# A hybrid encoder: q and k prepared for two token tiles at once, and GpSimd's large products given to VectorE

## The chip, the cores and the metric

The kernel runs on one core of a Trainium2 chip. The metric is the device time of the whole program in microseconds (us). A core has five engines that matter here, each with its own queue that it works through in order: TensorE (PE in the profile: matrix products and transposes; PEld is its loading of weights), VectorE (DVE), ScalarE (ACT), GpSimd (POOL) and SyncE (SP), which issues all of this kernel's transfers between HBM and the on-chip memory SBUF. TensorE writes its results into PSUM, from where VectorE and ScalarE read them.

## The reference, cut to what matters

Two layers act on a residual stream x of 512 tokens by 1024 columns, all in float32. A layer normalizes x, scales and shifts it by vectors made from the conditioning c, and multiplies it by w_in (1024 x 3712). The columns of that product feed three branches:

- A, differential attention: 4 heads with two softmax maps each over 32 columns of q and k, 64 columns of values;
- B, dilated window attention: 6 heads of 64 columns, with the three windows folded into one mask over 512 keys;
- C, retention: 4 heads, 48 columns of q and k, 96 of values, in chunks of 128 tokens, in both directions.

Each branch is multiplied by a SiLU gate, the three are joined and multiplied by w_out, and the result, times a gate made from c, is added to x. What the change touches is above all the preparation of q and k in A and B:

```
qa = rope(rms_norm(qa.reshape(B, S, H_A, 2, DK_A), qn_a[l]), ROT_THETA, ROT_A)
qb = rope(rms_norm(qb.reshape(B, S, H_B, DH_B), qn_b[l]), ROT_THETA, ROT_B)
```

That is: a root mean square over each head's 32 or 64 columns, a division by it, and a rotation of the first quarter of the columns. k goes the same way.

## The kernel before, in words

**Tiling.** The tokens lie in 4 tiles of 128 (`NT`), one token to a partition. Weights come in pieces of two blocks of 128 rows (`Piece`). Each is split into two parts whose sum is the float32 number: ScalarE writes the first part (`whi`), VectorE subtracts to get the second (`wlo`, L307), and three products replace one (`products`, L329). Products of one chunk of columns go group by group: one group is one weight piece with one token tile, six products; 16 groups make a chunk (`in_chunk`, L419) with four accumulating PSUM buffers, one for each token tile.

**The units.** A and B are worked through in units of two or four heads with 128 columns of q, of k and of values (`Unit`, L573): A0, B0, A1, B1, B2 in each layer, so 10 units in all, 4 of A (32 columns, 8 heads of q and k in a tile) and 6 of B (64 columns, 4 in a tile). When the 16 groups of a unit's chunk end, `done` (L580) copies q and k of a token tile into a buffer `qkraw` of 256 columns. Then three steps follow for each token tile:

- `norm` (L601): ScalarE squares the tile into `qkn`; VectorE sums each head (L608) and brings in 1/n and the epsilon (L570); GpSimd raises to the power -1/2 (L198, reached through `rms_end` and `pow_half`). VectorE forms two rotary products (L616, L617) and their sum (L618), in place in `qkraw`.
- `scale` (L620): GpSimd multiplies the 256 columns by the powers, broadcast over the head, into `qkn` (L622).
- `turn` (L625), for two tiles at once: TensorE transposes four blocks of 128x128 into the one PSUM buffer for turns (`tr4`, L552), ScalarE and VectorE empty it into `nat`.

When all four tiles are done, `stack` (L638) moves `nat` by transfers into the layout in which the scores read q and k. `Attention` (L665) and its two kinds, `Diff` (L704) and `Dilated` (L771), then make scores, Exp, softmax weights, turns of these and the products with the values; `finish2` to `finish4` (L743 to L769) end a unit of A: turn back, square (L748, GpSimd), sum, power, scaling (L762), gating (L764, GpSimd), turn again.

**Retention.** `rope` (L891) forms one rotary product on GpSimd (L896), one on VectorE (L898), and the sum on GpSimd (L899); `sums` and `norm` (L960, L965) take sums, power and scaling.

**The end of a layer.** `out_done` (L1110) multiplies a tile of the output product by the gate and adds x: in layer 0 on GpSimd for the first half of the columns and on VectorE for the second (L1117). `h_all` (L1087) makes the next layer's input, two pieces of 256 columns at a time.

**What sets the order.** The author's plan is a list of groups (`groups`), each of which may have steps bound to it (`at`, L163): a step named at group g is written behind group g's products. The constants in L33 to L51 are distances in groups: `NORM` 1, `SCALE` 5, `TURN` 6 after the last group of a token tile. This gives the order in which the program is written. The framework then makes each engine's queue: the order written is its priority, but an instruction that it takes to be ready may be put ahead of an earlier one. Two places are held: `high_priority` around the products with the values, and `tc.keep_in_program_order` in `sums` and `norm` of retention, which ties an instruction behind the one written before it on its engine. Once made, a queue is fixed, and an instruction that waits holds up everything behind it on its engine.

**Buffers.** A pool gives each tag a number of buffers. `qkraw` has 4 of 256 columns; the norm gains of the next layer (`mod_gain`, L477) share them. `qkn` has two tags with 2 each, which `h_tile` (L562) shares.

Of the kernel before, what the change touches and what calls it, by code (L numbers as in the profile page):

```python
# [48 lines left out]
E_T1, E_T2, E_X, E_QF, E_SCALE_A, E_SCALE_B = 1, 1, 1, 0, 0, 0  # L49
# [84 lines left out]
def encoder(ctx, tc, x, c, norm_g, w_ada, b_ada, w_in, w_out, params, consts, out):  # L134
# [5 lines left out]
    four = pool("four", 4)  # L140
# [421 lines left out]
    def h_tile(t, q, rstd):  # L562
        f = slice(q * 256, q * 256 + 256)
        hn = two.tile([P, 256], F32, name="hn", tag=f"qkn{q % 2}")
        stt(hn, x_sb[t][:, f], rstd[t], mods[q][:, 256:], OP.mult, OP.mult)
        V.tensor_tensor(hn, hn, mods[q][:, :256], OP.add)
        return hn
# [5 lines left out]
    class Unit:  # L573
# [6 lines left out]
        def done(self, t, ps, g0):  # L580
            if t == 0:
                self.v = three.tile([P, NT, P], F32, name="v")
                if self.gated:
                    self.ga = two.tile([P, NT, P], F32, name="ga")
            n, ng_ = self.n, 256 // self.n
            raw = self.raw[t] = four.tile([P, 256], F32, name="qkraw")
            act(raw, ps[:, 0:256])
            act(self.v[:, t], ps[:, 256:384])
            if self.gated:
                th = one.tile([P, P], F32, name="th")  # L590
                act(th, ps[:, 384:512], AF.Tanh, scale=0.5)
                stt(self.ga[:, t], th, 1.0, ps[:, 384:512], OP.add, OP.mult)
            g = g0 + 12 + t
            at(g + NORM, self.norm, t)
            at(g + SCALE, self.scale, t)
            if t % 2:
                at(g + TURN, self.turn, t // 2)
            if t == NT - 1:
                at(g + STACK, self.stack)

        def norm(self, t):  # L601
            n, ng_ = self.n, 256 // self.n
# [8 lines left out]
            ct_, st_ = tabs[n]  # L611
            r3 = raw.rearrange("p (g n) -> p g n", n=n)
# [7 lines left out]
        def scale(self, t):  # L620
            n, ng_ = self.n, 256 // self.n
            (V if (E_SCALE_A if n == DK_A else E_SCALE_B) % 2 else G).tensor_tensor(self.qn[t], self.raw[t].rearrange("p (g n) -> p g n", n=n),  # L622
                            self.ss[t].unsqueeze(2).to_broadcast([P, ng_, n]), OP.mult)

        def turn(self, i):  # L625
            if i == 0:
                self.nat = [[one.tile([P, S], F32R, name=f"nat{w}{z}", tag=f"nat{2 * w + z}") for z in range(2)] for w in range(2)]
            q2 = [self.qn[2 * i + j].rearrange("p g n -> p (g n)") for j in range(2)]
            ps = tr4([q2[j][:, w * P:(w + 1) * P] for w in range(2) for j in range(2)])
# [74 lines left out]
    class Diff(Attention):  # L704
# [38 lines left out]
        def finish2(self, g):  # L743
# [4 lines left out]
            G.tensor_tensor(sq, o, o, OP.mult)  # L748
# [10 lines left out]
        def finish3(self):  # L759
# [4 lines left out]
            G.tensor_tensor(on, on, self.u.ga, OP.mult)  # L764
# [6 lines left out]
    class Dilated(Attention):  # L771
        def __init__(self, unit, g0, gap, ob, sg, out):
            self.ob, self.sg, self.out = ob, sg, out
            self.s = {}
            super().__init__(unit, g0, gap, sg is not None)
# [6 lines left out]
        def scores(self, qt):  # L782
            for h in range(2):
# [7 lines left out]
                s_ = self.s[h] = sm.tile([P, 1], F32, name="bs")  # L791
                act(sb, sb, AF.Exp, bias=mx, scale=-1.0, accum_out=s_)

        def soft(self, qt):
            for h in range(2):
                V.reciprocal(self.s[h], self.s[h])
                sb = self.e[qt, h]
                if h == 0 or qt >= N_SOFT:
                    act(sb, sb, AF.Copy, scale=self.s[h])
                else:  # L800
                    V.tensor_scalar(sb, sb, self.s[h], None, OP.mult)
# [28 lines left out]
    class Retention:  # L830
# [60 lines left out]
        def rope(self, t):  # L891
# [22 lines left out]
        def turn_f(self, t):  # L914
            (V.tensor_copy if E_QF % 2 else act)(self.qfT[:, :, tok_(t)], tr4([self.fq[:, h] for h in range(4)]))
# [69 lines left out]
    def layer(l):  # L985
# [101 lines left out]
        def h_all(t, q):  # L1087
            hn = [h_tile(t, q + j, rstd_next) for j in range(2)]
            ps = tr4([hn[j][:, k * P:(k + 1) * P] for j in range(2) for k in range(2)])
# [8 lines left out]
        for hf in range(2):  # L1098
# [11 lines left out]
            def out_done(t, ps, cols, hf):  # L1110
# [5 lines left out]
                else:  # L1116
                    (V if hf * E_X % 2 else G).tensor_tensor(x_sb[t][:, cols], y, x_sb[t][:, cols], OP.add)  # L1117
# [181 lines left out]
```

## Time and profile before

| What | us |
|---|---|
| median of 3 runs (lowest, highest) | 652.2 (651.58, 652.81) |
| the profiled execution's own time | 653.0 |
| its span, first to last instruction | 651.2 |
| busy: PE | 625.5 |
| busy: PEld | 514.2 |
| busy: DVE | 496.8 |
| busy: ACT | 340.2 |
| busy: POOL | 164.4 |

The mean granted clock of TensorE is 0.989 of full speed. How to read the profile: "busy" is the time in which an engine had an instruction under way; an engine that is not the last to finish loses nothing by its idle time. A row of instructions names the source line, the engine, the operation, what is written and read, the shape (partitions x columns), the count, the busy time and the mean duration, then the idle time of the engine in front and who ended it. L155 and L158 are helpers through which many calls go; there the names of the tiles tell them apart. The chain of waits is followed back from the last instruction, at each step to what released it.

### The profile page before, as it was taken

The page shows a single profiled execution, that of the slowest core. Times are in us where ns is not written, and L with a number is a line of the kernel's source. Part 1 is how long each engine was busy: PE and PEld are TensorE (multiplying, and loading weights), DVE is VectorE, ACT ScalarE, POOL GpSimd, SP SyncE. Part 2 cuts the span into 40 slices and gives each one's busy share as a digit, 9 for nine tenths or more (in the row PEclk, how much of TensorE's full clock was granted, in tenths as well). Part 3 has the DMA queues.
Part 4 walks back from the last instruction along what each step waited for, and adds up shares of the span by engine and source line. Part 5 has one row for each costly group of instructions (what it writes and reads, how often), then busy time and mean ns, then how long its engine had stood idle before and what let it go on. Part 6 is the DMA issues. An engine that isn't in the chain of part 4 may idle for free.

```text
span 651.2 us, 10473 instructions
## 1 busy us (share of the span) xinstructions
PE 625.5 (96%) x3487; PEld 514.2 (79%) x3487; DVE 496.8 (76%) x1212; ACT 340.2 (52%) x750; POOL 164.4 (25%) x183
## 2 busy tenths in 40 slices
PE   6999999999999996999999999999999999899997
PEld 1878888987888873677779998997788787677786
DVE  1889776789978986997869374778997996677543
ACT  4744362666746665564434244455756567656410
POOL 1105462514360510200411041632323340010000
PEclk9799999999999998999999999999999999999999
DMA  9987123426565557476643322235555453603211
GB/s 315 334 290 207 40 82 88 133 91 152 147 177 167 125 172 175 141 254 224 185 169 96 90 72 67 77 101 154 142 171 137 142 142 103 163 32 139 89 64 65
DMA packets 87133, 93.03 MB, mean 143 GB/s; under 512 B 7044, under 2 KB 68132, under 8 KB 87080
## 3 DMA queue, kind: packets, MB, share of 16 engines
q1 hardware_dynamic: 87080, 92.37, 47.8%
q8 instruction: 28, 0.46, 0.3%
q14 instruction: 25, 0.20, 0.1%
HBM read 72.42 MB, written 4.19 MB: 118 GB/s over the span
## 4 chain that ended last, share of the span: by engine, by line
PE 77%; DVE 11%; issue 5%; POOL 3%; DMA 2%; ACT 2%; SPq 0%; POOLq 0%; ACTq 0%; DVEq 0%
PE acc L338 15%; PE acc L340 15%; PE acc L339 15%; PE tr L555 8%; PE pv L701 5%; PE sc L724 2%; PE acc L334 2%; PE acc L335 1%; PE acc L336 1%; DVE ada_acc L158 1%; PE sc L785 1%; DVE wlo L307 1%; PE sc L786 1%; PE line L519 1%; PE co L954 1%
## 5 line engine op out<-in xcount | busy, mean ns | idle before, releaser
L338 PE MATMUL acc<-whi,hT 128*128 128x384 f32 (+1 forms) x424 | 155.1, 366 | 0.0
L339 PE MATMUL acc<-wlo,hT 128*128 128x384 f32 (+1 forms) x424 | 152.3, 359 | 0.0
L340 PE MATMUL acc<-whi,hL 128*128 128x384 f32 (+1 forms) x424 | 152.0, 358 | 0.0
L307 DVE TENSOR_TENSOR wlo<-raw,whi 128x384 fp32r<-128x384 f32 (+1 forms) x130 | 81.8, 658 | 27.0 <-ACT whi L155 26.7
L198 POOL TENSOR_TENSOR qkss<-qkss,nhalf 128x4 f32<-128x4 f32 (+1 forms) x40 | 52.6, 1316 | 128.3 <-DVE qkss L570 125.7
L338 PEld LDWEIGHTS acc<-whi,hT 128*128 128x128 f32 x424 | 79.9, 188 | 6.1
L340 PEld LDWEIGHTS acc<-whi,hL 128*128 128x128 f32 x424 | 79.8, 188 | 6.2
L339 PEld LDWEIGHTS acc<-wlo,hT 128*128 128x128 f32 x424 | 79.9, 188 | 5.5
L155 ACT ACTIVATE whi<-raw 128x768 fp32r<-128x768 f32 (+2 forms) x67 | 59.6, 890 | 36.8 <-PE acc L340 34.0
L158 DVE SCALAR_TENSOR_TENSOR ada_acc<-raw,cs,ada_acc 128x512 f32<-128x512 f32 x86 | 64.4, 750 | 7.1 <-DMA raw<-in_w_ada_dram 5.9
L155 ACT ACTIVATE e<-sc,mx 128x512 f32<-128x512 f32 x64 | 43.9, 688 | 35.8 <-DVE mx L726 17.2
L726 DVE TENSOR_REDUCE mx<-sc 128x1 f32<-128x512 f32 x64 | 43.5, 685 | 9.6 <-PE sc L724 9.1
L155 ACT ACTIVATE sb<-sb,mx 128x512 f32<-128x512 f32 x48 | 34.4, 717 | 20.5 <-DVE mx L790 20.2
L701 PE MATMUL pv<-pt,v 128*64 128x256 f32 x320 | 40.1, 394 | 0.6 <-DVE pt L691 0.5
L155 ACT ACTIVATE pt<-tr 128x512 f32<-128x512 f32 x40 | 23.8, 596 | 24.2 <-PE tr L555 24.1
L790 DVE CUSTOM_DVE_ANT_0 sb<-sc,cst 128x512 f32<-128x512 f32 x48 | 32.1, 684 | 5.4 <-PE sc L786 3.5
L555 PE MATMUL tr<-cst,sb 128*128 128x128 f32 x192 | 30.5, 282 | 5.3 <-DVE nat L158 2.2
L701 PEld LDWEIGHTS pv<-pt,v 128*64 128x64 f32 x320 | 21.7, 140 | 16.6 <-DVE pt L691 5.3
L555 PEld LDWEIGHTS tr<-cst,sb 128*128 128x128 f32 x192 | 22.1, 142 | 15.8 <-ACT pt L155 7.3
L691 DVE COPY pt<-tr 128x512 f32<-128x512 f32 x40 | 27.4, 684 | 8.4 <-PE tr L555 8.4
L622 POOL TENSOR_TENSOR qkn<-qkraw,qkss 128x256 f32<-128x256 f32 x40 | 30.4, 760 | 5.8 <-DVE qkraw L618 2.0
L724 PE MATMUL sc<-stk,stq 96*128 96x512 f32 x64 | 27.3, 434 | 0.9 <-ACT e L155 0.9
(293 smaller groups left out, 1368.9 us busy)
## 6 DMA issues: line engine op xcount, KB each, us to landing
raw<-in_w_ada_dram SPq DMA_DIRECT2D x64, 256.0 KB, 4.8
raw<-in_w_in_dram SPq DMA_DIRECT2D x48, 192.0 KB, 2.6
raw<-in_w_in_dram SPq DMA_DIRECT2D x24, 384.0 KB, 3.9
raw<-in_w_in_dram SPq DMA_DIRECT2D x32, 256.0 KB, 3.6
raw<-in_w_ada_dram SPq DMA_DIRECT2D x16, 512.0 KB, 5.4
raw<-in_w_out_dram SPq DMA_DIRECT2D x32, 256.0 KB, 2.8
x<-in_x_dram SPq DMA_DIRECT2D x8, 512.0 KB, 3.5
stB<-nat SPq DMA_DIRECT2D x32, 128.0 KB, 2.3
```

The source lines that it names most:

```text
L155: A.activation(o, i, f, **kw)
L158: V.scalar_tensor_tensor(o, a, s, b, op0, op1)
L198: G.tensor_tensor(o, i, nhalf[:, :n], OP.pow)
L307: V.tensor_tensor(l2[:, z], r2[:, z], h2[:, z].bitcast(F32), OP.subtract)
L338: T.matmul(ps, ah, hi[i], start=s_, stop=False)
L339: T.matmul(ps, ah, lo[i], start=False, stop=False)
L340: T.matmul(ps, al, hi[i], start=False, stop=e_)
L555: T.transpose(ps[:, i, :], b, ident)
L701: T.matmul(self.pv[h * 64:h * 64 + 64, i * 256:i * 256 + 256], self.u.v[:, k, h * 64:h * 64 + 64], self.pt[h][:, k], start=k == 0, stop=k ...
L724: T.matmul(ps, self.u.stq[0:96, m, tok_(qt)], self.u.stk[0:96, m], start=True, stop=True)
L726: V.tensor_reduce(mx, ps, AX.X, OP.max, negate=True)
L790: V.tensor_tensor_reduce(sb, ps, cst[:, m0:m0 + S], 1.0, 3e38, OP.add, OP.min, mx)
```

## The change

Three things are done. First, `norm` and `scale` of a unit take two token tiles at a time: `qkraw` and `qkn` are tiles of two times 256 columns with 2 buffers each (the pool of 4 is gone), both steps stand only behind every second token tile, at the same distances in groups, and a power takes 8 or 16 numbers a row. Second, GpSimd's products go to VectorE: the scaling, retention's rotary product and sum, the gating of A, the residual sum of layer 0's first half; the square in `finish2` goes to ScalarE. GpSimd keeps the powers, the memsets and the rotary tables. Third, the scaling is tied with `tc.keep_in_program_order` behind what is written before it on VectorE. Beside these, the two softmax sums of a tile in B lie in one buffer and take one reciprocal, and `h_all` uses one tile of two pieces.

```diff
-        g = four.tile([P, 256], F32, name="ng", tag="qkraw")
+        g = two.tile([P, 256], F32, name="ng", tag="qkraw")
...
-            raw = self.raw[t] = four.tile([P, 256], F32, name="qkraw")
-            act(raw, ps[:, 0:256])
+            if t % 2 == 0:
+                self.raw[t // 2] = two.tile([P, 2, 256], F32, name="qkraw")
+            act(self.raw[t // 2][:, t % 2], ps[:, 0:256])
...
-            at(g + NORM, self.norm, t)
-            at(g + SCALE, self.scale, t)
             if t % 2:
+                at(g + NORM, self.norm, t // 2)
+                at(g + SCALE, self.scale, t // 2)
                 at(g + TURN, self.turn, t // 2)
...
-        def norm(self, t):
-            n, ng_ = self.n, 256 // self.n
+        def norm(self, i):
+
+            n, ng_ = self.n, 512 // self.n
             rot, h = n // 4, n // 8
-            raw = self.raw[t]
-            qn = self.qn[t] = two.tile([P, ng_, n], F32, name="qkn", tag=f"qkn{t % 2}")
-            act(qn.rearrange("p g n -> p (g n)"), raw, AF.Square)
-            ss = self.ss[t] = sm.tile([P, 8], F32, name="qkss")[:, :ng_]
+            raw = self.raw[i].rearrange("p t (g n) -> p (t g) n", n=n)
+            qn = self.qn[i] = two.tile([P, ng_, n], F32, name="qkn")
+            act(qn, raw, AF.Square)
+            ss = self.ss[i] = sm.tile([P, 16], F32, name="qkss")[:, :ng_]
             V.tensor_reduce(ss, qn, AX.X, OP.add)
             rms_end(ss, ng_, n)
...
-            (V if E_T2 % 2 else G).tensor_tensor(t2.rearrange("p g (w h) -> p g w h", w=2), sw, st_[:, t].rearrange("p g (w h) -> p g w h", w=2), OP.mult)
-            (V if E_T1 % 2 else G).tensor_tensor(t1, r3[:, :, :rot], ct_[:, t], OP.mult)
-            V.tensor_tensor(r3[:, :, :rot], t1, t2, OP.add)
+            V.tensor_tensor(t2.rearrange("p g (w h) -> p g w h", w=2), sw, st_.rearrange("p g (w h) -> p g w h", w=2), OP.mult)
+            V.tensor_tensor(t1, raw[:, :, :rot], ct_, OP.mult)
+            V.tensor_tensor(raw[:, :, :rot], t1, t2, OP.add)
...
-            (V if (E_SCALE_A if n == DK_A else E_SCALE_B) % 2 else G).tensor_tensor(self.qn[t], self.raw[t].rearrange("p (g n) -> p g n", n=n),
-                            self.ss[t].unsqueeze(2).to_broadcast([P, ng_, n]), OP.mult)
+            tc.keep_in_program_order(V.tensor_tensor(self.qn[i], self.raw[i].rearrange("p t (g n) -> p (t g) n", n=n),
+                                                     self.ss[i].unsqueeze(2).to_broadcast([P, ng_, n]), OP.mult))
...
-            G.tensor_tensor(sq, o, o, OP.mult)
+            act(sq, o, AF.Square)
...
-            G.tensor_tensor(on, on, self.u.ga, OP.mult)
+            V.tensor_tensor(on, on, self.u.ga, OP.mult)
...
         def scores(self, qt):
+            self.s = sm.tile([P, 2], F32, name="bs")
...
         def soft(self, qt):
+            V.reciprocal(self.s, self.s)
             for h in range(2):
-                V.reciprocal(self.s[h], self.s[h])
...
-            G.tensor_tensor(t1.rearrange("p h (w n) -> p h w n", w=2), sw,
+            V.tensor_tensor(t1.rearrange("p h (w n) -> p h w n", w=2), sw,
...
-            G.tensor_tensor(self.qkp[:, :, :DK_C], raw, t1, OP.add)
+            V.tensor_tensor(self.qkp[:, :, :DK_C], raw, t1, OP.add)
...
-                    (V if hf * E_X % 2 else G).tensor_tensor(x_sb[t][:, cols], y, x_sb[t][:, cols], OP.add)
+                    V.tensor_tensor(x_sb[t][:, cols], y, x_sb[t][:, cols], OP.add)
```

In the old lines the engine is chosen by constants of L49: `E_T1`, `E_T2` and `E_X` are 1, the others 0, so VectorE (`V`) has the two rotary products and GpSimd (`G`) the scaling.

## Rows read from the trace of the kernel before

**Rows 1.** The page, busy us, share of the span and instructions of each engine.

```profile
...
PE 625.5 (96%) x3487; PEld 514.2 (79%) x3487; DVE 496.8 (76%) x1212; ACT 340.2 (52%) x750; POOL 164.4 (25%) x183
...
```

**Rows 2.** TensorE's waits: engine, what it made, whom it waited for, us, times, longest.

```profile
...
PE tr L555 <- DVE nat L158: 3.4, 2, 2.2
...
PE sc L785 <- ACT e L155: 1.5, 2, 0.9
...
PE sc L785 <- ACT gate L155: 0.6, 1, 0.6
...
```

**Rows 3.** The chain that ended last, 186 to 198 us: start, us, what.

```profile
...
188.26 1.65 POOL oass L198
...
190.75 2.12 DVE wlo L307 x2
...
194.71 0.50 PE sc L785
...
```

**Rows 4.** The timeline, 158.9 to 162.8 us: start, us, instruction, [idle before, releaser].

```profile
...
159.03 1.63 POOL L198 TENSOR_TENSOR qkss<-qkss,nhalf 128x8 f32<-128x8 f32 x1
159.07 0.57 DVE L307 TENSOR_TENSOR wlo<-raw,whi 128x384 fp32r<-128x384 f32 x1
...
160.74 0.77 POOL L622 TENSOR_TENSOR qkn<-qkraw,qkss 128x256 f32<-128x256 f32 x1
...
160.96 1.77 DVE L158 SCALAR_TENSOR_TENSOR e<-e,rr 128x512 f32<-128x512 f32 x2
...
162.21 0.63 PE L555 MATMUL tr<-cst,e 128*128 128x128 f32 x4 [0.57 <-DVE e L158]
...
```

**Rows 5.** The timeline, 266.9 to 273 us, same columns.

```profile
...
270.14 1.27 POOL L764 TENSOR_TENSOR oao<-oao,ga 128x512 f32<-128x512 f32 x1
...
271.45 0.60 ACT L155 ACTIVATE gate<-ada_ps 128x512 f32<-128x512 f32 x1 [1.50 <-POOL oao L764]
...
```

**Rows 6.** Stretches of 20 us: PE, PEld, DVE, ACT, POOL busy, clock, DMA.

```profile
...
240.00:260.00 20.00, 14.81 (x82) 10.09 (x80) 14.83 (x36) 10.09 (x22) 0.43 (x1) 0.91 0.70 182
...
```

**Rows 7.** The page's groups: line, engine, operation, count | busy us, mean ns | idle.

```profile
...
L198 POOL TENSOR_TENSOR qkss<-qkss,nhalf 128x4 f32<-128x4 f32 (+1 forms) x40 | 52.6, 1316 | 128.3 <-DVE qkss L570 125.7
...
L622 POOL TENSOR_TENSOR qkn<-qkraw,qkss 128x256 f32<-128x256 f32 x40 | 30.4, 760 | 5.8 <-DVE qkraw L618 2.0
...
```

**Rows 8.** VectorE's groups by line and shape, the same columns.

```profile
...
L307 DVE TENSOR_TENSOR wlo<-raw,whi 128x384 fp32r<-128x384 f32 x90 | 50.6, 589 | 14.4 <-ACT whi L155 14.2
...
L307 DVE TENSOR_TENSOR wlo<-raw,whi 128x512 fp32r<-128x512 f32 x40 | 31.2, 813 | 12.5 <-ACT whi L155 12.5
...
L608 DVE TENSOR_REDUCE qkss<-qkn 128x4 f32<-128x256 f32 x24 | 9.8, 409 | 0.0
...
L898 DVE TENSOR_TENSOR craw<-craw,rc 128x384 f32<-128x384 f32 x8 | 6.7, 855 | 1.3 <-POOL ct L896 1.3
...
L616 DVE TENSOR_TENSOR rt<-qkraw,ropebs 128x64 f32<-128x64 f32 x24 | 6.1, 252 | 1.2 <-ACT qkraw L155 1.1
...
L968 DVE TENSOR_TENSOR cno<-cno,css 128x384 f32<-128x384 f32 x8 | 4.4, 550 | 0.0
...
L570 DVE TENSOR_SCALAR qkss<-qkss 128x4 f32<-128x4 f32 x24 | 4.3, 180 | 0.0
...
L762 DVE TENSOR_TENSOR oao<-oao,oass 128x512 f32<-128x512 f32 x4 | 2.8, 690 | 0.1
...
```

**Rows 9.** ScalarE's groups by shape, the same columns.

```profile
...
L155 ACT ACTIVATE junk<-x 128x512 f32<-128x512 f32 x8 | 5.0, 630 | 10.1 <-DVE x L1117 6.8 <-POOL x L1117 3.3
...
```

**Rows 10.** Line 198, GpSimd's powers: ns shortest, median, longest; starts; shapes.

```profile
...
L198 POOL TENSOR_TENSOR css<-css,nhalf x8: 1006/1007/1498, 112.1 to 432.4; 128x4 f32<-128x4 f32 x8
L198 POOL TENSOR_TENSOR oass<-oass,nhalf x4: 1635/1754/1878, 188.3 to 572.0; 128x8 f32<-128x8 f32 x4
...
```

**Rows 11.** The timeline, 95 to 104.3 us.

```profile
...
95.50 0.15 DVE L570 TENSOR_SCALAR qkss<-qkss 128x8 f32<-128x8 f32 x1
...
103.50 0.63 PE L555 MATMUL tr<-cst,qkn 128*128 128x128 f32 x4 [1.15 <-DVE nat L158]
...
```

More of the change, by code (lines that the diff above doesn't have):

```diff
@@ L48 @@
 N_A1, N_B1, N_SOFT = 5, 5, 9
-E_T1, E_T2, E_X, E_QF, E_SCALE_A, E_SCALE_B = 1, 1, 1, 0, 0, 0
 FIN2, FIN3, FIN4 = 4, 12, 16
@@ L139, in encoder @@
     three = pool("three", 3)
-    four = pool("four", 4)
     rp = pool("raw", 5)
@@ L560, in split, with h_tile @@
         V.tensor_tensor(lo, src, hi.bitcast(F32), OP.subtract)
-    def h_tile(t, q, rstd):
+    def h_tile(hn, t, q, rstd):
         f = slice(q * 256, q * 256 + 256)
-        hn = two.tile([P, 256], F32, name="hn", tag=f"qkn{q % 2}")
         stt(hn, x_sb[t][:, f], rstd[t], mods[q][:, 256:], OP.mult, OP.mult)
         V.tensor_tensor(hn, hn, mods[q][:, :256], OP.add)
-        return hn
     def rms_end(s, n, width):
@@ L599, in done @@
                 at(g + STACK, self.stack)
-        def norm(self, t):
-            n, ng_ = self.n, 256 // self.n
+        def norm(self, i):
+            n, ng_ = self.n, 512 // self.n
             rot, h = n // 4, n // 8
-            raw = self.raw[t]
-            qn = self.qn[t] = two.tile([P, ng_, n], F32, name="qkn", tag=f"qkn{t % 2}")
-            act(qn.rearrange("p g n -> p (g n)"), raw, AF.Square)
-            ss = self.ss[t] = sm.tile([P, 8], F32, name="qkss")[:, :ng_]
+            raw = self.raw[i].rearrange("p t (g n) -> p (t g) n", n=n)
+            qn = self.qn[i] = two.tile([P, ng_, n], F32, name="qkn")
+            act(qn, raw, AF.Square)
+            ss = self.ss[i] = sm.tile([P, 16], F32, name="qkss")[:, :ng_]
             V.tensor_reduce(ss, qn, AX.X, OP.add)
             rms_end(ss, ng_, n)
-            ct_, st_ = tabs[n]
-            r3 = raw.rearrange("p (g n) -> p g n", n=n)
+            ct_, st_ = (z[:, 2 * i:2 * i + 2].rearrange("p t g r -> p (t g) r") for z in tabs[n])
             t1 = two.tile([P, ng_, rot], F32, name="rt1")
@@ L627, in turn @@
                 self.nat = [[one.tile([P, S], F32R, name=f"nat{w}{z}", tag=f"nat{2 * w + z}") for z in range(2)] for w in range(2)]
-            q2 = [self.qn[2 * i + j].rearrange("p g n -> p (g n)") for j in range(2)]
-            ps = tr4([q2[j][:, w * P:(w + 1) * P] for w in range(2) for j in range(2)])
+            q2 = self.qn[i].rearrange("p (t g) n -> p t (g n)", t=2)
+            ps = tr4([q2[:, j, w * P:(w + 1) * P] for w in range(2) for j in range(2)])
             o = slice(2 * i * P, (2 * i + 2) * P)
@@ L773, in __init__ @@
             self.ob, self.sg, self.out = ob, sg, out
-            self.s = {}
             super().__init__(unit, g0, gap, sg is not None)
@@ L790, in scores @@
                 V.tensor_tensor_reduce(sb, ps, cst[:, m0:m0 + S], 1.0, 3e38, OP.add, OP.min, mx)
-                s_ = self.s[h] = sm.tile([P, 1], F32, name="bs")
-                act(sb, sb, AF.Exp, bias=mx, scale=-1.0, accum_out=s_)
+                act(sb, sb, AF.Exp, bias=mx, scale=-1.0, accum_out=self.s[:, h:h + 1])
         def soft(self, qt):
+            V.reciprocal(self.s, self.s)
             for h in range(2):
-                V.reciprocal(self.s[h], self.s[h])
-                sb = self.e[qt, h]
+                sb, s_ = self.e[qt, h], self.s[:, h:h + 1]
                 if h == 0 or qt >= N_SOFT:
-                    act(sb, sb, AF.Copy, scale=self.s[h])
+                    act(sb, sb, AF.Copy, scale=s_)
                 else:
-                    V.tensor_scalar(sb, sb, self.s[h], None, OP.mult)
+                    V.tensor_scalar(sb, sb, s_, None, OP.mult)
         def finish(self, g):
@@ L914, in turn_f @@
         def turn_f(self, t):
-            (V.tensor_copy if E_QF % 2 else act)(self.qfT[:, :, tok_(t)], tr4([self.fq[:, h] for h in range(4)]))
+            act(self.qfT[:, :, tok_(t)], tr4([self.fq[:, h] for h in range(4)]))
         def state(self, t):
@@ L1087, in h_all @@
         def h_all(t, q):
-            hn = [h_tile(t, q + j, rstd_next) for j in range(2)]
-            ps = tr4([hn[j][:, k * P:(k + 1) * P] for j in range(2) for k in range(2)])
+            hn = two.tile([P, 2, 256], F32, name="hn", tag="qkn")
+            for j in range(2):
+                h_tile(hn[:, j], t, q + j, rstd_next)
+            ps = tr4([hn[:, j, k * P:(k + 1) * P] for j in range(2) for k in range(2)])
             split(hT[:, 2 * q:2 * q + 4, tok_(t)], hL[:, 2 * q:2 * q + 4, tok_(t)], ps)
```

4 lines of the change are left out of this document (2 added, 2 removed).

## The prediction

> **What bounds the kernel now.** I read the page first: TensorE is busy 625.5 of 651.2 us [rows 1]. What an edit on the other engines can win is therefore the 25.7 us in which TensorE stands idle, and not the busy time that it takes off them. The table of what TensorE waited for comes next. Its largest entry lies in the start, before any unit, which the change does not touch. The entries further in name VectorE and ScalarE, not GpSimd: 3.4 us for the second half of a turned q or k, 1.5 us in two waits for an Exp, the longest 0.9, and 0.6 us for the gate's copy [rows 2]. So GpSimd can matter only behind them, and for that I followed the chain and the timeline back from single gaps.
>
> Three of them lead to a large GpSimd product. The score product that starts at 194.71 has waited 0.9 us, the longest of the waits for an Exp; the chain runs back through two splits of VectorE (2.12 us together) to a power of GpSimd, 1.65 us, for which VectorE stood [rows 3], and beside these splits GpSimd ran the gating product of the first differential unit. At 160.96 two mixing operations take 1.77 us while GpSimd scales a q/k tile from 160.74, and a TensorE gap of 0.57 us ends with the first of them [rows 4]. At 270.14 the gating product takes 1.27 us on GpSimd, the gate's copy on ScalarE waits 1.50 us for it, and TensorE's 0.6 us wait for that copy is behind it [rows 2, 5]. These three make 0.9 + 0.57 + 0.6 = 2.1 us.
>
> The costliest stretch is another: from 240 to 260 us TensorE is busy 14.81 of 20 us, and the granted clock has a mean of 0.91 of the 2.4 GHz level [rows 6]. GpSimd works 0.43 us there. What waits is the single PSUM buffer for turns, emptied by ScalarE and VectorE in turn. The change does not touch that.
>
> **The change part by part.** *Scaling on VectorE.* It takes 40 GpSimd products at 760 ns, 30.4 us, off that engine [rows 7], and gives VectorE 20 products of 512 columns at 690 ns (L762's form) [rows 8], 13.8 us.
>
> *Preparing two tiles at once.* Per tile VectorE does a reduce (409 ns), a scalar step (180), and three rotary operations (L616's 252; L617 and L618 repeat the row) [rows 8]; 40 times 1.35 is 53.8 us. Now 20 times: a reduce of 512 columns, 0.69; the scalar step, 0.19; three rotary operations on 128 columns. The trace has none on 128 in this form: they cost no less than one old one (0.25) and no more than two (0.50). I take 0.31, nearer the lower end, since from 64 to 512 columns the price rises from 0.25 to 0.69 us, 1 ns a column. With the scaling, 20 times (0.69 + 0.19 + 0.93 + 0.69) = 50.0 us: VectorE ends 3.8 us lower though it has the scaling too (between 7.4 lower and 7.6 higher by these bounds).
>
> *Other products.* The rotary products of retention (16 of 384 columns, 0.55 as L968) add 8.8 us, gating and residual (8 at 0.69) 5.5, and 24 reciprocals fewer, priced as L570's step, take 4.3 off [rows 8]. The sum for VectorE is -3.8 + 8.8 + 5.5 - 4.3 = +6.2 us. Four squares go to ScalarE, 0.63 us each as its squares of 512 columns in L1123 take [rows 9], 2.5 us; its 40 squares of a q/k tile become 20 of double width, which cost at most as much as before. So ScalarE gains at most 2.5 us of work on an engine busy 52% of the span, and I price it at nothing.
>
> *What VectorE gets back.* A product with both inputs in SBUF gets slower while GpSimd runs a large product: 128x512 splits have a mean of 813 ns against 690 for L762's, which runs alone; 128x384 splits 589 against 550; L898 855 against 550 [rows 8]. That is 40 x 0.123 + 90 x 0.039 + 8 x 0.305 = 4.9 + 3.5 + 2.4 = 10.8 us that go, and mixing and the rotary sums should give some too, which I leave unpriced. Net, VectorE falls by 10.8 - 6.2 = 4.6 us. A power costs nothing of this kind: at 159.03 one of 1.63 us runs, and the split that starts at 159.07 beside it takes 0.57 [rows 4].
>
> The Trainium skill, page "SBUF — State Buffer", section "SBUF: two separate sides", calls the port that GpSimd and VectorE share an exclusive lock: who starts first holds it for its whole instruction. For the large products the trace agrees. For powers it does not: by the rule that split would have waited for the 1.63 us, and the powers that fall away below would give VectorE up to 9.6 us more. I go by the row, and by the rule the time would come out at most 1 us lower.
>
> *Powers.* The shortest take 1.01 us for 4 numbers a row and 1.64 for 8 [rows 10], 0.16 us for one more. A differential unit's pair now has 16 in one power: between 1.64 and 3.28, and by the slope 2.9 us. The 8 of these and 12 of 1.64 make 43 us instead of 52.6 [rows 7]. GpSimd has its large products gone and runs them at once. Cost: nothing, as long as nobody stands behind them.
>
> *The added wait.* The scaling is now in VectorE's queue, pinned behind what the plan has before it, and everything after it on VectorE (splits, maxima, mixing) waits with it for the power. Its cover is the plan: four groups of products between NORM and SCALE, five to TURN. In the trace the scalar step of the last tile of a unit starts at 95.50 and its turn at 103.50, 8.0 us later [rows 11], with the scaling one group before the turn. Square and reduce lie before that step, so 2.9 us of power have to fit into some 6. I take 0 for it; the upper bound is 8 x 2.9 + 12 x 1.64 = 43 us of VectorE standing, if there were no cover at all.
>
> *Buffers.* Two pair tiles take the place of four single ones, so a unit's raw pair waits for the scaling of the unit before, 16 groups back; the norm gains of the second layer use them too, after the last unit. The first tile of a pair waits one group for the second, but the turn waited for the second anyway. Both at 0.
>
> *What reaches the end.* The three gaps, 2.1 us, should close: the products beside them are gone, or are 0.69 on VectorE instead of 1.27 on GpSimd and a hand-over. Retention's stages have no TensorE gap to win. For the other waits on VectorE and ScalarE in the unit stages I take 0.4 us of gain. The sum is 2.5 us off the profiled execution's 653.0 us, to 650.5. The median of the runs is 652.2, 0.8 lower, so the prediction is 649.7. After the gaps close, the turns' buffer is late next, at the same places as before.
>
> **The rivals.** *(a) Nothing is won.* VectorE's relief is a few us in 650, spread over all stages; the queue before each gap holds other work too, and the gap ends with the next item. For it: behind the start the wait table does not name GpSimd. Against: three gaps that I followed. Time: 652.2, between 651 and 653.4.
>
> *(b) Slower: VectorE stands at the scaling.* Place: a pair of a differential unit, where the pinned scaling comes less than 2.9 us after the scalar step, because the queue's order is dealt anew and the power starts late behind the rotary tables on GpSimd. Today's case shows the rate: a 1.65 us power for which VectorE stood was followed by 0.9 us of TensorE gap [rows 2, 3], 0.55 us for each us. If half of the 8 pairs stood for the whole 2.9 us, it costs 4 x 2.9 x 0.55 = 6.4 us; with the 2.5 us won beside it the time is 649.7 + 6.4 = 656.1, and I put the case at 655.5. It decides from about 1.6 pairs on (1.6 x 2.9 x 0.55 = 2.5). Against it: 8.0 us of cover.
>
> *(c) More is won: the turns come at other times.* The turn of a q/k tile sits in the chain of 240 to 260; the longest wait for VectorE's half of it, 2.2 us [rows 2], is there. If the new order draws that turn out of the chain, the wait and 1.8 us of clock (0.09 of 20 us [rows 6]) go as well: 649.7 - 4.0 = 645.7. Nothing in the profile says that it will.
>
> **How the numbers follow.** The forecast has 0.48 (own range 648 to 651.5), (a) 0.20, (b) 0.20, (c) 0.12. What a measurement can tell from no change is 0.2%, 1.3 us. Faster than 650.9: most of the forecast (0.42) and (c), 0.54. Within: the rest of the forecast and nearly all of (a), 0.24. Slower than 653.5: (b) and an end of (a), 0.22. The range reaches to 645.0 for (c), and to 656.0 through most of (b).
>
> **What would show it.** Right: splits of 512 columns at 0.69 us on the mean; the gap before the score product near 194 and the gate's copy waiting for no gating product; 20 scalings near 0.69 us with no VectorE idle time before them; 16-number powers near 2.9 us. Wrong: VectorE idle before the scaling, released by a GpSimd power (b); VectorE relieved and TensorE's idle time unchanged (a); the stretch before the gates shorter (c). Should TensorE's busy time differ by more than the clock explains, the reading that only its idle time is open was wrong.

## The result

The changed kernel takes 661.9 us (median of 4 runs, 660.65 to 662.34) against 651.9 of the kernel before (4 runs, 650.54 to 652.81): a ratio of 1.0162 with a 95% interval of 1.0129 to 1.0194. It is 10 us slower, where the prediction was 649.7 us, faster, with a range up to 656.0.

The page of the changed kernel, busy us, share and instructions of each engine; its profiled execution took 662.3 us:

```profile
...
PE 630.4 (95%) x3487; PEld 518.3 (78%) x3487; DVE 493.3 (75%) x1132; ACT 342.2 (52%) x734; POOL 93.1 (14%) x95
...
```

Against [rows 1], GpSimd gives up 71.3 us and VectorE, which took its products over, still has 3.5 us less. TensorE executes the same 3487 instructions, is busy 4.9 us longer and idle more: adding up the idle time ahead of its instructions gives 26.6 us against 22.2. The two make the 9.3 us between the profiled executions. More busy time for the same instructions goes with a lower clock, as the next but one view shows.

What TensorE waited for in the changed kernel (us in total, times, longest):

```profile
...
PE tr L553 <- DVE nat L156: 3.5, 4, 1.9
PE acc L332 <- DVE cth L156: 2.4, 2, 1.2
PE tr L553 <- DVE qkn L619: 2.0, 2, 1.0
PE tr L553 <- DVE bs L791: 1.6, 1, 1.6
...
PE sc L721 <- ACT e L153: 1.2, 2, 0.9
...
```

The three waits that the prediction traced to GpSimd products, at 162.21, 194.71 and 272.10 [rows 2 to 5], are no longer in the list. New is the third line: a turn that waits for the scaling itself (`qkn`, L619). The wait for `cth`, which belongs to retention's gate, has grown from 0.6 to 2.4 us, and the joint reciprocal of B (`bs`) ends one of 1.6 us near 249, where the kernel before waited 2.2 us for `nat`. Waits of these two kinds are nearly as long with the scaling back on GpSimd (e3_scale_gpsimd, 2.0 and 1.65 us), so they don't come of the scaling.

Stretches of 20 us, the changed kernel (PE, PEld, DVE, ACT, POOL busy, clock, DMA share, GB/s):

```profile
...
240.00:260.00 20.00, 14.68 (x81) 10.06 (x79) 16.39 (x36) 11.84 (x25) 0.00 (x0) 0.91 0.77 208
260.00:280.00 20.00, 18.81 (x94) 14.07 (x93) 17.84 (x42) 12.21 (x27) 2.40 (x2) 0.91 0.46 138
...
560.00:580.00 20.00, 13.30 (x63) 8.46 (x64) 10.58 (x28) 9.60 (x21) 0.53 (x1) 0.79 0.42 106
...
```

and the kernel before at the last two of these places:

```profile
...
260.00:280.00 20.00, 18.97 (x99) 13.90 (x98) 18.87 (x44) 11.71 (x25) 4.34 (x4) 1.00 0.44 147
...
560.00:580.00 20.00, 17.34 (x95) 11.93 (x94) 13.33 (x35) 11.55 (x24) 4.20 (x3) 0.91 0.36 90
...
```

The stretch from 240 is as it was [rows 6]; in the one behind it, in the last part of layer 0's attention, the granted clock is 0.91 where it was 1.00. At 560, the end of the attention of layer 1, TensorE is busy 4.0 us less and has a mean granted clock of 0.79 of the 2.4 GHz level instead of 0.91. All engines are idler there, so something is being waited for that began earlier. Two comparisons of the traces say what. The first is when a group of attention's products with the values begins in layer 1 (us, ten groups), the second is the start of the k-th weight product, after minus before:

```
group      1     2     3     4     5     6     7     8     9     10
before   466.5 477.5 493.8 517.5 535.2 547.2 562.1 573.2 590.8 610.9
after    468.9 479.3 497.8 522.6 540.8 554.2 569.2 582.6 600.1 620.2
later      2.4   1.8   4.0   5.1   5.6   7.0   7.1   9.4   9.3   9.3

k            192  624  816  1440  1680  1776  1824  1920
after-before -0.3 -2.4 +1.2 +1.1  -4.0  -7.2  +9.4  +9.4
```

The attention of layer 1 begins 2.4 us late, a part that layer 0 leaves behind, and falls back further step by step, from the third group on. TensorE does not stand meanwhile: it runs its weight products sooner, until at product 1776 it is 7.2 us ahead with them. From 558.1 to 578.3 its queue then holds no weight product (before: from 560.0 to 569.0), and what is left there are the attention's turns, scores and products with the values, which wait for each other's exponentials and copies. At product 1824 the lead has become a lag of 9.4 us, and it stays. Most of it shows nothing where it is lost; it is paid at the end of the layer.

What fell back are the turns of q and k. In layer 1, unit A1 (the third to be prepared), the kernel before, GpSimd and then TensorE (start, us, instruction, [idle before, releaser]):

```profile
...
468.55 1.63 POOL L198 TENSOR_TENSOR qkss<-qkss,nhalf 128x8 f32<-128x8 f32 x1
470.25 0.62 POOL L622 TENSOR_TENSOR qkn<-qkraw,qkss 128x256 f32<-128x256 f32 x1
...
475.36 2.20 POOL L198 TENSOR_TENSOR qkss<-qkss,nhalf 128x8 f32<-128x8 f32 x1 [1.64 <-PE tr L555]
477.64 0.61 POOL L622 TENSOR_TENSOR qkn<-qkraw,qkss 128x256 f32<-128x256 f32 x1
...
479.41 0.66 PE L555 MATMUL tr<-cst,qkn 128*128 128x128 f32 x4
...
482.79 0.60 PE L555 MATMUL tr<-cst,qkn 128*128 128x128 f32 x4
...
```

and the changed kernel, GpSimd, VectorE and TensorE:

```profile
...
470.43 2.90 POOL L196 TENSOR_TENSOR qkss<-qkss,nhalf 128x16 f32<-128x16 f32 x1 [24.45 <-DVE qkss L566]
476.56 3.01 POOL L196 TENSOR_TENSOR qkss<-qkss,nhalf 128x16 f32<-128x16 f32 x1 [3.23 <-DVE qkss L566]
...
481.01 0.68 DVE L619 TENSOR_TENSOR qkn<-qkraw,qkss 128x512 f32<-128x512 f32 x1
...
482.74 0.69 DVE L619 TENSOR_TENSOR qkn<-qkraw,qkss 128x512 f32<-128x512 f32 x1
...
484.00 0.60 PE L553 MATMUL tr<-cst,qkn 128*128 128x128 f32 x4
...
487.85 0.60 PE L553 MATMUL tr<-cst,qkn 128*128 128x128 f32 x4
...
```

Before, the scaling starts less than 0.1 us after its power ends, on an engine with nothing else to do. After, the first pair's power ends at 473.33 and its scaling starts at 481.01: 7.7 us in which VectorE does the work that stands ahead of it, without a pause. In the kernel before, the first turn's second tile was scaled at 470.9, 8.5 us ahead of the turn; now the scaling ends at 481.7, 2.3 us after the turn's old time. The two turns come 4.6 and 5.1 us later, 2.4 of which is there already at the first group of this layer, before A1 is prepared. No bracket stands behind them, so TensorE did not wait: the first turn starts another 2.3 us after its scaling, and the order of TensorE's queue has other products there.

### The profile page after: what moved, and what is told of

Read it like the earlier page. It is cut to its first block, busy times and chain, and to the rows that moved or that the text cites. A ratio compares the mean times of both kernels' runs of the same rounds, so it can differ in the third digit from the quotient of the medians.

```text
span 660.5 us, 10196 instructions
## 1 busy us (share of the span) xinstructions
PE 630.4 (95%) x3487; PEld 518.3 (78%) x3487; DVE 493.3 (75%) x1132; ACT 342.2 (52%) x734; POOL 93.1 (14%) x95
## 4 chain that ended last, share of the span: by engine, by line
PE 87%; DVE 6%; ACT 3%; DMA 2%; issue 1%; SPq 0%; POOL 0%; ACTq 0%; DVEq 0%
PE acc L336 17%; PE acc L338 17%; PE acc L337 17%; PE tr L553 10%; PE pv L698 6%; PE sc L721 3%; PE acc L332 2%; PE acc L333 2%; PE acc L334 2%; DMA raw<-in_w_ada_dram 2%; PE sc L782 2%; PE sc L783 1%; DVE ada_acc L156 1%; PE line L517 1%; PE co L950 1%
## 5 line engine op out<-in xcount | busy, mean ns | idle before, releaser
L305 DVE TENSOR_TENSOR wlo<-raw,whi 128x384 fp32r<-128x384 f32 (+1 forms) x130 | 73.7, 596 | 27.6 <-ACT whi L153 27.4
L196 POOL TENSOR_TENSOR qkss<-qkss,nhalf 128x8 f32<-128x8 f32 (+1 forms) x20 | 46.6, 2332 | 213.4 <-DVE qkss L566 213.4
L553 PE MATMUL tr<-cst,sb 128*128 128x128 f32 x192 | 32.1, 293 | 9.7 <-ACT pt L153 4.0
L153 ACT ACTIVATE pt<-tr 128x512 f32<-128x512 f32 x40 | 23.8, 595 | 21.4 <-PE tr L553 21.4
L153 ACT ACTIVATE nat<-tr,gcol 128x256 fp32r<-128x256 f32 x40 | 19.0, 474 | 17.6 <-PE tr L553 12.7
```

The source lines that it names most:

```text
L153: A.activation(o, i, f, **kw)
L196: G.tensor_tensor(o, i, nhalf[:, :n], OP.pow)
L305: V.tensor_tensor(l2[:, z], r2[:, z], h2[:, z].bitcast(F32), OP.subtract)
L553: T.transpose(ps[:, i, :], b, ident)
```

## The experiments

In the expectations, each of which names its own theories, one view runs through all: that the scaling costs time because of its place in VectorE's queue. The others look for the cost in the buffers, in the longer powers of a pair, in the other moved products, or in an order that is dealt anew. Each ratio is against runs of the kernel before on the same chip.

### The tie

**e1_no_tie**: the scaling on VectorE, not tied.

```
- tc.keep_in_program_order(V.tensor_tensor(self.qn[i], ...))
+ V.tensor_tensor(self.qn[i], ...)
```

> The changed kernel with the scaling no longer tied to the plan. Theory T (the tie keeps the scaling in VectorE's queue for 8 to 20 us after its power has ended; the last unit's turns and the release of the raw pair come late, and TensorE runs out of products at the end of layer 1): the scalings start within some 4 us of their power's end, layer 1's last unit is turned by about 550 us, the time falls from 662 to 650 to 655 us. Rival P (preparing two tiles at once makes q and k late by itself): 659 to 662. Rival M (the products that came to VectorE draw its queue anew): 659 to 662. A new VectorE idle time of up to 2.9 us in front of each of the 8 differential scalings is what T has to pay.

Measured: 661.1 us, 1.0131 (1.0075 to 1.0186). The scaling's line, VectorE's idle time before it by releaser (us, times):

```profile
...
  POOL qkss L196: 18.8, 10
...
```

and the timeline at two of these cases, with what followed on TensorE:

```profile
...
94.37 0.69 DVE L619 TENSOR_TENSOR qkn<-qkraw,qkss 128x512 f32<-128x512 f32 x1 [2.90 <-POOL qkss L196]
...
101.87 0.69 DVE L619 TENSOR_TENSOR qkn<-qkraw,qkss 128x512 f32<-128x512 f32 x1 [2.71 <-POOL qkss L196]
...
108.06 0.64 PE L553 MATMUL tr<-cst,qkn 128*128 128x128 f32 x4 [4.62 <-DVE nat L156]
...
```

This is what the prediction's rival (b) describes, here and not in the changed kernel: VectorE stands for ten powers, 18.8 us, and behind one of these comes a TensorE gap of 4.62 us, where the kernel before has 1.15 [rows 11]. In the changed kernel VectorE's idle time before its 20 scalings is 0.0: with the tie there is no standing, and the scaling comes late instead. Both cost about the same, so theory T of this run failed: the tie is not what the loss needs.

**e8_scale3**: tied, two groups of products earlier.

```
- NORM, SCALE, TURN, STACK = 1, 5, 6, 6
+ NORM, SCALE, TURN, STACK = 1, 3, 6, 6
```

> The changed kernel with the scaling dealt two groups of products earlier (3 instead of 5 groups after the pair is in), tied there. Theory T: the scaling of the differential units comes 3 to 6 us earlier, but some of the powers, 2.9 us, are then not yet done and VectorE stands for them; 655 to 660 us, with VectorE idle before some scalings. If the place in VectorE's queue did not matter (E), 661 to 662 as the changed kernel.

Measured: 659.9 us, 1.0125 (1.0089 to 1.0161). VectorE's idle time before the scalings:

```profile
...
  POOL qkss L196: 6.8, 4
...
```

It has something of both, and its six runs reach from 654.9 to 663.0 us: some standing (one of 2.82 us), and scalings of A1 in layer 1 that start at 478.1 and 484.5. Its attention is late as well. No place in this queue that was tried is a good one.

### The buffers

**e2_three_raw**: three pairs of `qkraw`; to make room, the rotary products use one buffer instead of four.

```
- self.raw[t // 2] = two.tile([P, 2, 256], F32, name="qkraw")
+ self.raw[t // 2] = three.tile([P, 2, 256], F32, name="qkraw")
```

> The changed kernel with three raw pair buffers instead of two (room made by one rotary buffer fewer and the first rotary product in place), tie kept. If the tie harms through the buffers (the last unit's third and fourth tile wait for the scaling of the unit before, and two accumulators are held 7 to 10 us): those copies come 7 to 10 us sooner and the time falls to 653 to 657 us. If it harms through the late turn alone: 660 to 663, with the copies sooner all the same. P and M: 660 to 663.

Measured: 660.4 us, 1.0140 (1.0096 to 1.0183). In the changed kernel, the copies of the third and fourth tile of B2 in layer 1 wait until B1's scaling at 528.3 has released the pair (529.0 and 529.4). Here they run at 517.7 and 519.8, with no wait, and B2's scalings still start at 550.6 and 559.5 (554.0 and 561.6 in the changed kernel). The wait for the buffer is real, and without it the time is the same within the intervals.

### Scaling back on GpSimd

**e3_scale_gpsimd**: pairs, long powers, all moved products stay; only the scaling goes back, untied.

```
- tc.keep_in_program_order(V.tensor_tensor(self.qn[i], ...))
+ G.tensor_tensor(self.qn[i], ...)
```

> The changed kernel with the scaling of two tiles on GpSimd and untied; all else as changed. T: the scaling follows its power at once, 649 to 654 us. P: 659 to 662, since pairs and the long power are kept. M: 658 to 662, since the other moved products stay on VectorE.

Measured: 653.7 us, 1.0038 (1.0010 to 1.0065). Of the 10 us, 8 are gone: the loss comes with the scaling's move to VectorE; without it the other parts cost little. GpSimd's scalings and powers (count | busy us, mean ns | idle):

```profile
...
L619 POOL TENSOR_TENSOR qkn<-qkraw,qkss 128x512 f32<-128x512 f32 x20 | 24.4, 1219 | 2.4 <-ACT th L153 1.1
L196 POOL TENSOR_TENSOR qkss<-qkss,nhalf 128x16 f32<-128x16 f32 x8 | 24.3, 3036 | 116.6 <-DVE qkss L566 116.6
...
```

A scaling is nearly twice as long there as VectorE's 0.69 us, and the kernel faster. The turns of A1 in layer 1 start at 476.1 and 479.3.

**e5_one_unit_gpsimd**: the changed kernel, with the scaling of one of the ten units, A1 of layer 1, on GpSimd.

```
+ if self.key in ((1, "A", 1),): G.tensor_tensor(*z)
+ else: tc.keep_in_program_order(V.tensor_tensor(*z))
```

> The changed kernel with the scaling of one unit alone, A1 of layer 1, on GpSimd and untied; the other nine stay tied on VectorE. Theory Q (the scaling waits for its place in a VectorE queue that is full in the unit stages, whether tied or not; the q and k of a unit come some 5 us late, and the attention behind it slips while TensorE spends its products early): this unit's turns come 4 to 5 us sooner (about 479 and 483 us instead of 484.0 and 487.8), the attention behind it by as much, and the time falls by 3 to 6 us, to 656 to 659. Rival E (the loss arises at the end of layer 1, at the last unit's own scaling, whatever came before): 660 to 663.

Measured: 655.5 us, 1.0057 (1.0028 to 1.0086): this one unit gives back 6 of the 10 us. Its GpSimd from 466 to 480 us:

```profile
...
467.79 2.90 POOL L196 TENSOR_TENSOR qkss<-qkss,nhalf 128x16 f32<-128x16 f32 x1 [24.48 <-DVE qkss L566]
470.76 1.05 POOL L621 TENSOR_TENSOR qkn<-qkraw,qkss 128x512 f32<-128x512 f32 x1
...
477.60 1.05 POOL L621 TENSOR_TENSOR qkn<-qkraw,qkss 128x512 f32<-128x512 f32 x1
...
```

and the stretch at the end of layer 1:

```profile
...
560.00:580.00 20.00, 15.91 (x89) 10.94 (x88) 13.07 (x33) 10.23 (x24) 1.88 (x1) 0.91 0.38 93
...
```

The turns start at 479.1 and 482.5, as before the change; the attention's groups are within 1.0 us of the kernel before up to the seventh; and 80 us later the clock is at 0.91 again. Up to this unit's scalings, near 481 us of the changed kernel, TensorE, VectorE, ScalarE and GpSimd have the same instructions in the same order in both kernels, so what this run gives back is lost behind that point.

**e6_a_units_gpsimd**, **e6_b_units_gpsimd**: the four units of A, or the six of B, on GpSimd.

```
+ if n == DK_A: G.tensor_tensor(*z)      # e6_b: n != DK_A
```

> The changed kernel with the scaling of the 4 differential units on GpSimd and untied, that of the 6 dilated units tied on VectorE. Q: half of the loss or more comes back, 653 to 658 us. E: the last units are dilated and keep their tie, 659 to 663.

> The reverse: dilated units' scaling on GpSimd and untied, differential units' tied on VectorE. E: 651 to 655 us. Q: between, 654 to 659, since the slip of A1 is kept and those of B1 and B2 are not.

Measured: 656.1 us, 1.0063 (1.0034 to 1.0092), and 657.4 us, 1.0086 (1.0055 to 1.0117). Four units of A give no more than A1 of layer 1 alone. The six of B give back about 5 us though A1 stays late (its turns at 480.1 and 483.6, not as late as in the changed kernel), so the units' shares don't add up.

**e10_two_units_gpsimd**: A1 and B2 of layer 1.

```
+ if self.key in ((1, "A", 1), (1, "B", 2)): G.tensor_tensor(*z)
```

> The changed kernel with the scaling of two units of layer 1 on GpSimd and untied, the second differential and the third dilated; the other eight units keep it on VectorE, tied. Theory T: these are the units whose late turns the end of the layer waits for, so it goes as with all ten on GpSimd, 653 to 655 us (one of them alone had 655.5). If what remains of the loss lies spread over all units (rival S), 655 to 656.5, as with the one.

Measured: 656.8 us, 1.0080 (1.0060 to 1.0101); both numbers of the expectation missed low. B2's scalings move from 546.7 and 555.4 (with A1 alone) to 533.0 and 536.8, and its turns start no earlier for it: 551.1 and 558.3 against 548.8 and 556.5. Up to these scalings the two kernels have the same queues, and this execution has been 2.0 us behind the other since its first 40 us, so the turns are at the same place in both. Once A1 is in time, B2's late scaling is not what its turn waits for.

### Parts of the change on the kernel before

**e4_moves_only**: the kernel before with the gating, retention's rotary products and the residual on VectorE and the square on ScalarE; q and k as before.

```
- G.tensor_tensor(on, on, self.u.ga, OP.mult)
+ V.tensor_tensor(on, on, self.u.ga, OP.mult)     (and four more lines of this kind)
```

> The kernel before with only the other products moved: retention's rotary product and sum, the gating and the residual to VectorE, the square to ScalarE; single tiles, scaling on GpSimd. T: no harm, 649 to 653 us, with the gate's copy waiting for no gating product. M: 657 to 662. P says nothing here beyond T.

Measured: 653.4 us, 1.0021 (0.9990 to 1.0051): no harm, and none of the gain that the prediction counted on. The gaps at 194 and at the gate are closed, 1.57 us; the one of 0.57 us at 162 stays, as GpSimd's scaling does here; but the wait for `cth` near 260 grows from 0.31 to 1.19 us, one of 0.56 us at 508 is 0.85 now, and TensorE's idle time falls from 22.2 to 21.4 us only.

**e7_single_dve**: the kernel before with the scaling of single tiles on VectorE, untied.

```
- E_T1, E_T2, E_X, E_QF, E_SCALE_A, E_SCALE_B = 1, 1, 1, 0, 0, 0
+ E_T1, E_T2, E_X, E_QF, E_SCALE_A, E_SCALE_B = 1, 1, 1, 0, 1, 1
```

> The kernel before with nothing changed but the engine of the scaling: single tiles, VectorE, untied. Q: the same loss without pairs and without tie, 656 to 664 us, and VectorE's busy time some 17 us above the kernel before. If the pairs are needed for the loss: 651 to 654.

Measured: 654.9 us, 1.0043 (1.0015 to 1.0071). VectorE's idle time before the 40 scalings:

```profile
...
  POOL qkss L198: 9.7, 14
...
```

It costs, but less than expected. The power, the scaling and the turn of the second tile of A1 in layer 1:

```profile
...
467.06 1.64 POOL L198 TENSOR_TENSOR qkss<-qkss,nhalf 128x8 f32<-128x8 f32 x1 [2.16 <-DVE qkss L570]
...
477.60 0.41 DVE L622 TENSOR_TENSOR qkn<-qkraw,qkss 128x256 f32<-128x256 f32 x1
...
478.31 0.66 PE L555 MATMUL tr<-cst,qkn 128*128 128x128 f32 x4
...
```

This scaling waits 8.9 us after its power, longer than in the changed kernel, and still ends at 478.0, just ahead of its turn; the turns are in time (478.3 and 482.2). So a long wait in VectorE's queue costs nothing by itself while the power comes early enough. The tie isn't needed for the rest of the changed kernel's loss (e1_no_tie); what this run lacks beside it are the pairs, with their later and longer power, the other moved products and the joint reciprocal. Single tiles scaled on VectorE together with these were not run, so the pair as the missing part is argued and not shown.

### The lateness by itself

The experiments so far move work between engines, and so the order of all queues with it. These two leave the kernel before as it is and only make one scaling late: powers with the exponent 1, on GpSimd, ahead of the second tile's scaling in A1 of layer 1.

```
+ if self.key == (1, "A", 1) and t == 1:
+     for _ in range(7):                      # e9_late_3: 3
+         G.tensor_tensor(self.ss[t], self.ss[t], expo1[:, :ng_], OP.pow)
```

> The kernel before, with seven powers with the exponent 1 (8 numbers a row, 1.64 us each, 11.5 us on GpSimd) between the power and the scaling of the second tile of the second differential unit of layer 1. Nothing is added to VectorE; scaling stays on GpSimd. The scaling of that tile should move from 470.3 to some 481 us and the two behind it to 483 and 485, about where the changed kernel has them, so that the unit's two turns start near 482 and 487 instead of 479.4 and 482.8. Theory (T: a late scaling in this one unit costs by itself, because scores, attention and all units after it wait for the turn): 656 to 659 us, attention from then on 3 to 5 us late. Rival (E: the loss comes of the whole order being dealt anew by other instructions on VectorE, and the late scaling only stands beside it): within 0.2% of the kernel before, 652 to 653.5.

> The same with three such powers, 4.9 us: the scaling of that tile ends near 476 us, those behind it near 478.5 and 481, all before the turn that needs them (479.4 and 482.8 in the kernel before). Both theories expect no change, 651.5 to 653.5; if T is right in substance but the time is lost before the turn already, it would be 654 or more.

Measured: with seven 657.6 us, 1.0098 (1.0077 to 1.0118); with three 651.1 us, 0.9994 (0.9973 to 1.0014). But for the added powers, and the one fill of their exponents, every engine has the same instructions in the same order as in the kernel before. With seven, GpSimd and TensorE:

```profile
...
469.63 13.10 POOL L626 TENSOR_TENSOR qkss<-qkss,expo 128x8 f32<-128x8 f32 x7
482.80 0.62 POOL L627 TENSOR_TENSOR qkn<-qkraw,qkss 128x256 f32<-128x256 f32 x1
...
483.48 0.90 PE L557 MATMUL tr<-cst,qkn 128*128 128x128 f32 x3 [4.47 <-POOL qkn L627]
...
484.49 0.52 PE L341 MATMUL acc<-wlo,hT 128*128 128x384 f32 x1
...
489.01 0.60 PE L557 MATMUL tr<-cst,qkn 128*128 128x128 f32 x4
...
```

and with three:

```profile
...
468.71 5.63 POOL L626 TENSOR_TENSOR qkss<-qkss,expo 128x8 f32<-128x8 f32 x3
474.42 1.03 POOL L627 TENSOR_TENSOR qkn<-qkraw,qkss 128x256 f32<-128x256 f32 x1
...
477.75 0.66 PE L557 MATMUL tr<-cst,qkn 128*128 128x128 f32 x4
...
481.11 0.60 PE L557 MATMUL tr<-cst,qkn 128*128 128x128 f32 x4
...
```

The scaling that ends before its turn's place in the queue (475.4, turn at 477.8) costs nothing, though the three added powers took 5.6 us. The one that ends later, behind seven powers of 13.1 us together, costs its lateness: 4.47 us of gap, the slower products behind it, and 6.0 us in the time, with VectorE's work unchanged. That makes lateness of this unit a cause by itself. The way is another than in the changed kernel: here TensorE stands for the scaling, there it does not, since its queue was made with the turn at a later place. That the 6.0 us are also what the unit gave back in e5_one_unit_gpsimd is therefore no measure of the one by the other.

## Why the prediction was wrong

**The step that failed** is "*The added wait.* ... I take 0 for it". It asked one question only: who stands behind the scaling while this waits for its power. It set 2.9 us of power against some 6 of the 8.0 us of cover [rows 11] and found room. The term at 0 was worth some 8 us: that much comes back when only the scaling leaves VectorE's queue (e3_scale_gpsimd). The other question was not asked: how long the scaling, now an entry of VectorE's queue, waits for its turn there after the power is done, and who waits for the scaling. VectorE is busy 18.18 of 20 us from 460 to 480 (19.51 before); the answer in A1 of layer 1 is 7.7 us for the first pair and 3.2 for the second. With the power and the scaling the first pair needs 2.9 + 7.7 + 0.7 = 11.3 us, and starts 1.9 us later than the second tile did before, as the whole program is 2.4 us late by then; there the way from power (468.55) to turn was 10.9 us, of which power and scaling took 2.3. Over all 20 pairs the time between power and scaling is 1.6 to 25.0 us, longest in B1; A1 of layer 1, which gave back most, has one of the shorter ones. So its length alone does not decide, but the room that the turn leaves for it. Behind the scaling are the turn, the stack, the scores and every later unit. GpSimd's idle 75% [rows 1] was no waste here: it was the reason that the scaling came less than 0.1 us after its power.

```profile
...
460.00:480.00 20.00, 20.00 (x116) 15.48 (x116) 18.18 (x44) 13.21 (x35) 5.91 (x2) 1.00 0.66 171
...
```

**Rival (b)** had the right sign and the wrong place: VectorE doesn't stand before a scaling in the changed kernel. Its price, 655.5, was for half of eight pairs and a gap at once; the real loss was paid for the most part at the end of layer 1, with the clock, and is larger.

**The signs of being right** that the prediction named all came: the splits' price, 20 scalings near 0.69 us with no idle time before them, powers near 2.9 us, the gaps closed. None of them asks when the scaling is done, so all four hold in a kernel that is 10 us slower.

**The sizes of VectorE's work were right.** VectorE's groups of the changed kernel, by line and shape:

```profile
...
L305 DVE TENSOR_TENSOR wlo<-raw,whi 128x384 fp32r<-128x384 f32 x90 | 47.2, 553 | 14.5 <-ACT whi L153 14.4
L305 DVE TENSOR_TENSOR wlo<-raw,whi 128x512 fp32r<-128x512 f32 x40 | 26.5, 693 | 13.1 <-ACT whi L153 13.0
L619 DVE TENSOR_TENSOR qkn<-qkraw,qkss 128x512 f32<-128x512 f32 x20 | 13.7, 687 | 0.0
L605 DVE TENSOR_REDUCE qkss<-qkn 128x8 f32<-128x512 f32 x12 | 8.2, 681 | 0.3 <-ACT qkn L153 0.2
L614 DVE TENSOR_TENSOR qkraw<-rt,rt 128x128 f32<-128x128 f32 x20 | 5.7, 283 | 0.0
...
L894 DVE TENSOR_TENSOR craw<-craw,rc 128x384 f32<-128x384 f32 x8 | 4.3, 553 | 0.1
...
```

The split of 512 columns falls from 813 to 693 ns, that of 384 from 589 to 553, L898's product (L894 now) from 855 to 553 [rows 8]: 40 x 0.120 + 90 x 0.036 + 8 x 0.302 = 10.5 us, predicted 10.8. VectorE has 493.3 us, predicted 492.2. A power of 16 numbers takes 2.90 us where nothing lengthens it, as estimated; all 20 take 46.6 us, not 43, since some are longer (up to 3.48). The Trainium skill's rule of an exclusive lock ("SBUF — State Buffer", section "SBUF: two separate sides") stays answered as the prediction had it: with the large products gone the splits have nearly their price alone, and powers don't hold VectorE up: in the changed kernel 17 splits ran beside a power and took 0.69 and 0.55 us on the mean, as they do alone.

**The relief reached nothing.** Rival (a) is what happened to the 2.5 us: e4_moves_only closes two of the three gaps and TensorE's idle time falls by 0.8 us, the measured time not at all (1.0021, 0.9990 to 1.0051). The term of 2.5 us was wrong with this: no run shows a gain, and other waits grew in place of the closed ones; the prediction's own last sentence on the gaps said this of the turns' buffer, and did not price it.

**The buffers** at 0 were right in the time (e2_three_raw), though the wait itself was there.

**What stays open.** Giving A1 of layer 1 back to GpSimd returns 6 of the 10 us. How much of this is the lateness of its turns and how much the other order that the queues take behind it was not separated. The rest belongs to the other units: with all ten on GpSimd about 8 of 10 come back, with A1 and B2 no more than with A1. A part of the rest has a place. Up to A1 of layer 1 the changed kernel, e5_one_unit_gpsimd and e10_two_units_gpsimd have the same queues, and from product 192 to the first group of layer 1 they lose 2.7, 1.7 and 1.7 us against the kernel before. With the four units of A on GpSimd it is 2.0, with the six of B there they gain 0.4. So about 2 us seem to be lost before A1 of layer 1 and to go with the scaling of B; through which wait was not followed. Single executions leave such sums open by about 1 us: the two e9 kernels, which have the queues of the kernel before up to there, differ from it by +0.5 and -0.9. Executions of the same queues also part in their first 40 us, by up to 2.0 us, and nearly keep that distance. Differences of 1 to 2 us between runs (e5_one_unit_gpsimd and e10_two_units_gpsimd) may be no more than that. What of the 1.6 us left in e3_scale_gpsimd is the pairing, the moved products or the joint reciprocal was not separated. No version is clear of noise faster than the kernel before.

## What to carry to other kernels

Before moving a step to a busier engine, ask not only whom it will hold up there but how long it will stand in that queue itself, and put this against the slack of the one who reads its result: here 7.7 us of queue, and a power longer by 1.3, against 8.5 us between the old scaling and its turn. With single tiles 8.9 us of queue were still in time (e7_single_dve). An engine busy 25% may be worth its slow products because it is ready at once. And when idle time appears far from the edit, compare when the k-th product and the k-th step of the dependent chain start in both traces: look for the cause where they begin to part, beyond the distance with which the two executions leave the start; the gap may be only where it is paid.

## What was not expected of the hardware

After the gap of 4.47 us in e9_late_7 the granted clock was 0.50 of the 2.4 GHz level, that is the 1.2 GHz level, from 484 to 488 us, with TensorE busy throughout:

```profile
...
484.00:488.00 4.00, 4.00 (x13) 3.61 (x12) 2.43 (x5) 1.44 (x3) 3.84 (x4) 0.50 0.16 31
...
```

A product of 384 columns took 0.52 us there against 0.34 later. The queues are those of the kernel before, so the two traces can be compared product by product: the lag grows by 6.8 us here, 4.5 of it the gap and the rest with the clock, and 1.2 us come back by the end of the layer. GpSimd's scaling of 512 columns took 1.05 us at its shortest, less than two of 256 at 0.61, and 1.22 on the mean.
